# Neighbour sums by one-hot products: second pass in groups of four, its running counts on GpSimd, and keys read from PSUM

## The chip, the cores and the metric

One core of one Trainium2 chip. The metric is the device time of one execution in microseconds, the median over runs. Engines are called by the names of the profile: PE is TensorE's matmul side, PEld its weight loads, DVE VectorE, ACT ScalarE, POOL GpSimd, SP the engine that issues most DMAs.

## What is computed

A graph has 4096 nodes with 128 features each and 65536 edges. Each edge adds the features of its source node to the output row of its destination node:

```python
num_nodes, num_edges, dim = 4096, 65536, 128
output = np.zeros((num_nodes, dim), dtype=np.float32)
for i in range(len(edge_index_src)):
    output[edge_index_dst[i]] += node_features[edge_index_src[i]]
```

Source and destination indices are drawn at random. In and out are float32.

## The kernel before

The output is cut into 32 blocks of 128 destination nodes, the features into 32 blocks of 128 source nodes. The kernel sorts the edges by destination block and then by source block, so that each pair of blocks gets 128 edge places or a fixed part of them, and builds from the sorted edges a 128 x 128 matrix of counts for each pair. The output is then a sum of plain matrix products: counts times features. `_fast` (L79) holds all of it, in an order written out by hand; every engine runs its instructions in that order.

**Pass 1** (L312 to L492) sorts by destination block. The edges come as 24 chunks (NCH) by 22 (NJ), in six quarters q of four chunks. For a quarter, `oh1s` (L208) compares keys with a row of numbers and gives one-hots over 32 blocks; `counts` (L227) makes running counts with matmuls and ScalarE and gathers each edge's rank; `spread1` (L257) multiplies the one-hots by two payloads, the code of the edge (k = 0) and its source block (k = 1); `move1` (L275) builds a one-hot of the ranks on VectorE and multiplies it, on PE, with the spread payloads, so that each edge moves to its rank. The spread tile v1 has two buffers, used in turn by the quarters. `onehot` (L197) is the helper of all these comparisons, so they stand under L200 in the profile; its first operand (`piota`, `piotas`) lies in PSUM, in the tile `psi`. The first four destination blocks of the second pass are prepared beside the quarters (`beside`, L432). `x_part` (L182) splits the features in two parts that are multiplied separately: ScalarE rounds one, GpSimd subtracts for the other.

**Pass 2** (`pass2`, L506) sorts the edges of a group of destination blocks by source block. GROUPS gives the groups: 4, 4, 4, 4, 8 and 8 destination blocks. A group of four makes bucket one-hots (`buckets4`, one VectorE instruction), column sums, scans, and counts with 24 matmuls and six ScalarE passes (`counts_ranks`, L621). A group of eight makes them with 32 small VectorE instructions (`buckets`), sums on PE over all chunks before (`before_all`), 11 dependent VectorE additions (`running`, L553) and 12 GpSimd products (`masked`, L560). Both gather ranks with 32 matmuls (`ranks`), build permutations on VectorE (`permutations`) and apply them on PE to payloads that GpSimd multiplied (`payload`, `permuted`). ScalarE then takes the sorted keys out of PSUM (`take_pairs`, L408) to an SBUF tile `pa`, and VectorE extracts from it source and destination within the block (`put_keys`, L416, two instructions at L421). `little` hands out the GpSimd products, seven to a slot.

**The slots** (L720 to L746), one for each destination block, run beside that. In slot n VectorE makes the one-hots of slot n + 1 (`onehots`, L650: 2 x 4096 elements), PE multiplies this slot's one-hots to blocks of counts (`blocks`, L660: 8 of 4 matmuls each, in four PSUM buffers `psa`), ScalarE casts each to SBUF (L665), and PE multiplies the blocks of the slot before with the features (`product`, L667: 8 of 2 matmuls). After every fourth slot `evacuate` and `finish` (L295 to L310) copy the result out of PSUM, transpose it on PE and send it to HBM. STEPS says which steps of which group are taken in which slot; a step's first function runs after the one-hots, its second at the slot's end, its third two slots later.

```python
        for k0 in (0, 4):
            for k in range(k0, k0 + 4):
                blocks(k, cur, a)
            if k0 == 4:
                finish()
            if prev is not None:
                for k in range(k0, k0 + 4):
                    product(k, *prev)
```

Of the kernel before, what the change touches and what calls it, by code (L numbers as in the profile page):

```python
# [25 lines left out]
GROUPS = (4, 4, 4, 4, 8, 8)  # L26

STEPS = {0: (1, 2), 1: (1,), 2: (2,), 3: (3,), 4: (2,), 5: (3, 2), 6: (4,), 7: (4,), 8: (3,),
         9: (3,), 10: (4,), 12: (4,), 13: (4,), 14: (5,), 15: (5,), 16: (4,), 17: (4,), 18: (5,),
         20: (5,), 21: (5,), 24: (5,), 25: (5,)}  # L30
# [48 lines left out]
def _fast(ctx, tc, X, src32, dst32, out, ident, fmax, flag_i, T):  # L79
# [52 lines left out]
    psi = ps.tile([P, 4, P // 2], I32, name="psi", tag="psi", bufs=1)  # L132
# [124 lines left out]
    def spread1(q):  # L257
# [224 lines left out]
    for q in range(NQ):  # L482
# [15 lines left out]
    small = []  # L498

    def little(n=0, until=None):  # L500
        while small and (n > 0 or any(k == until for k, _ in small)):
            small.pop(0)[1]()
            n -= 1


    def pass2(g):  # L506


        d0, gd = first[g], GROUPS[g]
        kk = 4 if gd % 4 == 0 else 2  # L510
        gk = gd // kk
        shape = [P, NCH, gk, NB, kk]
        W = NB * gd
        T2 = {}

        def flat2(t):
            return t.rearrange("p c i s k -> p c (i s k)")

        def tiles():
            at = -(g - 1) % 3  # L520
            tags = ("c0", "o1", "o0")
            T2["o"] = sb1.tile(shape, BF16, name="oh2", tag=tags[at])[:]
            T2["c"] = sb1.tile(shape, BF16, name="cum2", tag=tags[(at + 1) % 3])[:]
            T2["v"] = sb1.tile(shape, BF16, name="v2", tag="F" if g % 2 == 0 else "c1")[:]

        def buckets():
            tiles()
            ds = slice(d0, d0 + gd)
            for s in range(NB):
                V.tensor_single_scalar(  # L530
                    out=T2["o"][:, :, :, s, :], scalar=float(s + 1), op=OP.is_equal,
                    in_=sbk[:, :, ds].rearrange("p c (i k) -> p c i k", k=kk))

        def before_all():
            psb = ps.tile([P, 512], F32, name="psb", tag="misc", bufs=1)
            for h in range(2):
                for c in range(NH):
                    PE.matmul(out=psb[:, h * W:(h + 1) * W], lhsT=before[:],
                              rhs=flat2(T2["o"])[:, h * NH + c], start=c == 0, stop=c == NH - 1)
            for h in range(2):  # L540
                S.copy(out=flat2(T2["c"])[:, h * NH], in_=psb[:, h * W:(h + 1) * W])  # L541

        def payload(i, cs):
            ds = slice(d0 + kk * i, d0 + kk * i + kk)
            G.tensor_tensor(out=T2["v"][:, cs, i], in0=T2["o"][:, cs, i], op=OP.mult,  # L545
                            in1=sa[:, cs, None, ds].to_broadcast([P, cs.stop - cs.start, NB, kk]))

        def payloads():
            for i in range(gk):
                for c in range(0, NCH, 4):  # L550
                    small.append(((g, 1), lambda i=i, c=c: payload(i, slice(c, c + 4))))

        def running():  # L553
            cums = flat2(T2["c"]).rearrange("p (h c) w -> p h c w", h=2)
            ohs2 = flat2(T2["o"]).rearrange("p (h c) w -> p h c w", h=2)
            for c in range(1, NH):
                V.tensor_tensor(out=cums[:, :, c], in0=cums[:, :, c - 1], in1=ohs2[:, :, c - 1],  # L557
                                op=OP.add)

        def masked():  # L560
            for c in range(0, NCH, 2):
                small.append(((g, 0), lambda c=c: G.tensor_tensor(  # L562
                    out=flat2(T2["c"])[:, c:c + 2], in0=flat2(T2["c"])[:, c:c + 2],
                    in1=flat2(T2["o"])[:, c:c + 2], op=OP.mult)))

        def ranks():
            little(until=(g, 0))
            psr = ps.tile([P, 512], F32, name="psr2", tag="misc", bufs=1)
            for s in range(NB):
                PE.matmul(out=psr[:, :NCH * gd], lhsT=identb[:],  # L570
                          rhs=T2["c"][:, :, :, s, :].rearrange("p c i k -> p (c i) k"),
                          start=s == 0, stop=s == NB - 1)
            T2["r"] = sb2.tile([P, gd // 2, NCH, 2, 2], BF16, name="rank2")
            for k in range(2):
                S.copy(out=T2["r"][:, :, :, :, k],
                       in_=psr[:, :NCH * gd].rearrange("p (c j u) -> p j c u", j=gd // 2, u=2))

        def permutations(i):
            pair_onehot(p2b[(d0 + i) // 2 % 4], T2["r"][:, i // 2], slice(0, NCH))

        def permuted(i):
            little(until=(g, 1))
            if i % 4 == 0:
                T2["ps2"] = ps.tile([P, 512], F32, name="ps2", tag="ps2", bufs=1)
            ps2 = T2["ps2"]
            for c in range(NCH):
                at = (c // NH * 2 + i % 4 // 2) * 64
                PE.matmul(out=ps2[:, at:at + 64], lhsT=p2b[(d0 + i) // 2 % 4][:, c, :],  # L588
                          rhs=T2["v"][:, c, i // kk, :, i % kk:i % kk + 2],
                          start=c % NH == 0, stop=c % NH == NH - 1)  # L590
            if i % 4 == 2:
# [250 lines left out]
```

## Time and profile before

| | us |
|---|---|
| median of 3 runs | 336.03 (334.42 to 336.85) |
| the profiled execution | 334.62 |
| its span, first to last instruction | 332.6 |
| PE busy | 280.8 (84%) |
| DVE busy | 283.4 (85%) |
| ACT busy | 199.8 (60%) |
| POOL busy | 94.7 (28%) |

The profile is of one execution. Busy time is the time in which an engine has an instruction at work; PE's ends are modelled, and POOL's are rough. Pass 1 goes to about 84 us of the span, the slots from about 90 to 327. DMA moves 5.76 MB and is busy almost only in the first 20 us. The mean granted clock of TensorE was 0.957 of 2.4 GHz.

### The profile page before, as it was taken

The page shows a single profiled execution, that of the slowest core. Times are in us where ns is not written, and L with a number is a line of the kernel's source. Part 1 is how long each engine was busy: PE and PEld are TensorE (multiplying, and loading weights), DVE is VectorE, ACT ScalarE, POOL GpSimd, SP SyncE. Part 2 cuts the span into 40 slices and gives each one's busy share as a digit, 9 for nine tenths or more (in the row PEclk, how much of TensorE's full clock was granted, in tenths as well). Part 3 has the DMA queues.
Part 4 walks back from the last instruction along what each step waited for, and adds up shares of the span by engine and source line. Part 5 has one row for each costly group of instructions (what it writes and reads, how often), then busy time and mean ns, then how long its engine had stood idle before and what let it go on. Part 6 is the DMA issues. An engine that isn't in the chain of part 4 may idle for free.

```text
span 332.6 us, 8069 instructions
## 1 busy us (share of the span) xinstructions
PE 280.8 (84%) x3488; PEld 235.0 (71%) x3496; DVE 283.4 (85%) x335; ACT 199.8 (60%) x411; POOL 94.7 (28%) x102
## 2 busy tenths in 40 slices
PE   0579868666739989899689999985999999999994
PEld 0468757656638778688478888864888888888882
DVE  4999999977899839958999899999989969968800
ACT  2776545311735867865547578562657787787761
POOL 6634021110606070003999000189920000000000
PEclk9999999969878999999979999995999999999999
DMA  8500000000000000100001001000100100100101
GB/s 240 138 2 5 2 3 2 2 2 2 2 3 0 2 3 0 34 3 0 2 0 34 2 0 34 0 2 1 34 2 0 34 2 0 34 0 3 34 1 32
DMA packets 8708, 5.76 MB, mean 17 GB/s; under 512 B 224, under 2 KB 8416, under 8 KB 8672
## 3 DMA queue, kind: packets, MB, share of 16 engines
q1 hardware_dynamic: 8528, 4.72, 5.0%
q8 instruction: 27, 0.44, 0.6%
q10 hardware_dynamic: 144, 0.52, 0.5%
q14 instruction: 9, 0.07, 0.1%
HBM read 3.15 MB, written 2.10 MB: 16 GB/s over the span
## 4 chain that ended last, share of the span: by engine, by line
PE 51%; DVE 36%; issue 6%; ACT 4%; DMA 1%; DVEq 0%; ACTq 0%
PE pso L670 27%; PE psa L663 14%; DVE oh L200 12%; DVE p L200 6%; DVE v L261 5%; DVE cum L557 5%; PE ps L588 3%; PE psr L570 3%; ACT cum L631 2%; DMA raw<-in_edge_index_dst_dram 1%; DVE p2a L200 1%; DVE oh L530 1%; PE psm L285 1%; DVE oh L602 1%; DVE p2c L200 1%
## 5 line engine op out<-in xcount | busy, mean ns | idle before, releaser
L665 ACT CAST a<-psa 128x512 fp32r<-128x512 f32 x256 | 131.6, 605 | 48.9 <-PE psa L663 48.3
L670 PE MATMUL pso<-a,xr 128*128 128x512 f32 x512 | 135.0, 406 | 0.0
L670 PEld LDWEIGHTS pso<-a,xr 128*128 128x128 f32 x512 | 93.0, 191 | 17.2
L200 DVE TENSOR_TENSOR oh<-psi,slo 128x4096 bf16<-128x4096 uint16 (+1 forms) x33 | 73.3, 2221 | 20.2 <-PE psa L663 20.1
L200 DVE TENSOR_TENSOR oh<-psi,dlo 128x4096 bf16<-128x4096 uint16 (+1 forms) x33 | 73.1, 2216 | 0.0
L663 PE MATMUL psa<-oh 128*128 128x128 bf16 x1024 | 70.8, 224 | 0.5 <-DVE oh L200 0.3
L663 PEld LDWEIGHTS <-oh 128*128 128x128 bf16 x1024 | 60.2, 100 | 12.0 <-issue 10.9
L545 POOL TENSOR_TENSOR v<-oh,sa 128x512 bf16<-128x512 bf16 x42 | 42.6, 1054 | 35.2 <-DVE oh L602 35.2
L562 POOL TENSOR_TENSOR cum<-cum,oh 128x512 bf16<-128x512 bf16 x24 | 29.5, 1252 | 65.8 <-DVE cum L557 65.8
L200 DVE TENSOR_TENSOR p<-psi,rank 128x448 bf16<-128x448 uint16 (+3 forms) x72 | 29.7, 474 | 0.0
L240 ACT ACTIVATE cum<-psc,minus 128x512 bf16<-128x512 f32 (+1 forms) x36 | 21.4, 653 | 11.8 <-PE psc L237 11.7
L285 PE MATMUL psm<-v,p 128*128 128x64 bf16 x512 | 20.8, 197 | 2.1 <-DVE p L200 1.8
L588 PE MATMUL ps<-v,p2c 128*128 128x64 bf16 x192 | 8.7, 209 | 14.1 <-DVE p2c L200 14.1
L285 PEld LDWEIGHTS <-p 128*128 128x128 bf16 x512 | 18.4, 101 | 2.8 <-DVE p L200 2.6
L588 PEld LDWEIGHTS <-p2c 128*128 128x128 bf16 x192 | 7.6, 107 | 16.5 <-DVE p2c L200 15.2
L557 DVE TENSOR_TENSOR cum<-cum,oh 128x512 bf16<-128x512 bf16 x22 | 16.1, 732 | 1.5 <-ACT cum L541 0.8
L189 POOL TENSOR_TENSOR xr<-xf,xr 128x512 fp32r<-128x512 f32 x8 | 11.9, 1519 | 12.9 <-ACT xr L185 12.9
L358 POOL TENSOR_TENSOR vc<-oh,sa 128x512 bf16<-128x512 bf16 x5 | 5.2, 1048 | 33.9 <-DVE oh L353 33.9
L200 DVE TENSOR_TENSOR p2a<-psi,rank 128x3072 bf16<-128x3072 uint16 (+2 forms) x14 | 14.5, 1062 | 0.2 <-ACT rank L390 0.2
L215 PE MATMUL pst<-ones,oh 128*128 128x1 bf16 x132 | 4.3, 164 | 12.0 <-DVE oh L200 12.0
L237 PE MATMUL psc<-identb,sums 128*128 128x128 bf16 x126 | 13.9, 234 | 0.4 <-issue 0.2
L237 PEld LDWEIGHTS <-sums 128*128 128x128 bf16 x126 | 11.1, 106 | 4.5 <-issue 1.4
(94 smaller groups left out, 278.1 us busy)
## 6 DMA issues: line engine op xcount, KB each, us to landing
xf<-in_node_features_dram SPq DMA_DIRECT2D x4, 512.0 KB, 7.4
out_dram<-rows SPq DMA_DIRECT2D x8, 256.0 KB, 2.3
raw<-in_edge_index_src_dram ACTq DMA_DIRECT2D x1, 512.0 KB, 4.7
raw<-in_edge_index_dst_dram SPq DMA_DIRECT2D x1, 512.0 KB, 5.0
```

The costliest lines, as they stand in the source:

```text
L200: V.tensor_tensor(out=dst.rearrange("p i (m k) -> p i m k", k=2), in0=io.rearrange("p i (m k) -> p i m k", k=2), in1=keys2[:, :, None, :]. ...
L237: PE.matmul(out=psc[:, (j - j0) * P:(j - j0 + 1) * P], lhsT=sums[q][:, j - 1:j].to_broadcast([P, P]), rhs=identb[:], start=False, stop=j = ...
L240: S.activation(out=cum[:, :, 4 * j0:4 * (j0 + n)], func=RELU, bias=minus[:], in_=psc[:, :n * P].rearrange("p (t b) -> p b t", b=NB))
L261: V.tensor_tensor(out=v1[q][:, :, k, :].rearrange("p t (b k) -> p t b k", k=2), in0=oh1q(q).rearrange("p t (b k) -> p t b k", k=2), in1=ke ...
L285: PE.matmul(out=psm[:, l * 64:(l + 1) * 64], lhsT=t[:, l % 2, j, :], rhs=v1[q][:, 4 * j + l].rearrange("p k b -> p (k b)"), start=j == 0, ...
L545: G.tensor_tensor(out=T2["v"][:, cs, i], in0=T2["o"][:, cs, i], op=OP.mult, in1=sa[:, cs, None, ds].to_broadcast([P, cs.stop - cs.start, N ...
L557: V.tensor_tensor(out=cums[:, :, c], in0=cums[:, :, c - 1], in1=ohs2[:, :, c - 1], op=OP.add)
L562: small.append(((g, 0), lambda c=c: G.tensor_tensor(out=flat2(T2["c"])[:, c:c + 2], in0=flat2(T2["c"])[:, c:c + 2], in1=flat2(T2["o"])[:, ...
L588: PE.matmul(out=ps2[:, at:at + 64], lhsT=p2b[(d0 + i) // 2 % 4][:, c, :], rhs=T2["v"][:, c, i // kk, :, i % kk:i % kk + 2], start=c % NH = ...
L663: PE.matmul(out=psa[:, i * P:(i + 1) * P], lhsT=oh[:, 0, 4 * k + i, :], rhs=oh[:, 1, 4 * k + i, :], start=True, stop=True)
L665: S.copy(out=a[:, k, :], in_=psa[:])
L670: PE.matmul(out=pso[:], lhsT=xr[s // 16][:, s % 16, v, :], rhs=a[:, k, :], start=s == 0 and v == 0, stop=s == NB - 1 and v == 1)
```

## The change

- Pass 1: `spread1` is split. `spread_blocks` multiplies the source blocks (k = 1) on GpSimd, four instructions of 22 x 32 elements a quarter. `spread_codes` keeps the codes (k = 0) on VectorE; it first copies the quarter's keys, as 88 fp32 words, to PSUM (`pkey`) and reads them from there. The subtraction of the third part of the features moves behind the first two `spread_blocks` in GpSimd's order.
- The PSUM tile of `psi` becomes a full bank. Behind the numbers for the comparisons lie `pkey` and two buffers `pa`.
- `take_pairs` writes the sorted keys as fp32 to `pa` in PSUM, and `put_keys` reads the upper 16 bits of each word there.
- Pass 2: eight groups of four. Group 0 is made in pass 1 as before, group 1 with column sums and counts as before, groups 2 to 7 with one bucket instruction, `before_all`, 11 additions of 2 x 128 elements (`running`, now on GpSimd), six masks of 512 and six payloads of 512, all on GpSimd and given out at once. `little` goes.
- STEPS: group g from 3 on takes its steps in slots 4g - 9 (buckets, sums), 4g - 8 (running, masked, payloads), 4g - 6 (ranks), 4g - 4 and 4g - 3 (permutations); its keys are extracted in slot 4g - 1, where the one-hots of slot 4g are made.
- The slots: the products of a slot's first four groups of blocks follow its last four blocks, and those of its last four follow the next slot's first four blocks.

```diff
-GROUPS = (4, 4, 4, 4, 8, 8)
+GROUPS = (4,) * 8
+
+STEPS = {0: (2,), 1: (1, 1, 2), 3: (2,), 4: (2,), 5: (2,)}
+for _g in range(3, 8):
+    for _s in (4 * _g - 9, 4 * _g - 8, 4 * _g - 6, 4 * _g - 4, 4 * _g - 3):
+        STEPS[_s] = STEPS.get(_s, ()) + (_g,)
...
+    psib = ps.tile([P, 512], I32, name="psi", tag="psi", bufs=1)
+    psi = psib[:, :4 * P // 2].rearrange("p (n w) -> p n w", w=P // 2)
+    pkey = psib[:, 512 - 3 * 4 * NJ:].rearrange("p (n w) -> p n w", w=4 * NJ)
...
-        for k, key in ((0, kab), (1, kb[:])):
-            V.tensor_tensor(
-                out=v1[q][:, :, k, :].rearrange("p t (b k) -> p t b k", k=2),
-                in0=oh1q(q).rearrange("p t (b k) -> p t b k", k=2),
-                in1=key[:, q, :, None, :].to_broadcast([P, NL, NB // 2, 2]), op=OP.mult)
+        for l in range(4):
+            G.tensor_tensor(out=v1[q][:, l::4, 1, :], in0=oh1q(q)[:, l::4], op=OP.mult,
+                            in1=kb[:, q, l::4, :1].to_broadcast([P, NJ, NB]))
+
+    def spread_codes(q):
+
+        V.tensor_copy(out=pkey[:, q % 3].bitcast(F32),
+                      in_=ka[:, q].rearrange("p t k -> p (t k)").bitcast(F32))
+        V.tensor_tensor(
+            out=v1[q][:, :, 0, :].rearrange("p t (b k) -> p t b k", k=2),
+            in0=oh1q(q).rearrange("p t (b k) -> p t b k", k=2), op=OP.mult,
+            in1=pkey[:, q % 3].bitcast(BF16).rearrange("p (t k) -> p t k", k=2)[:, :, None, :]
+            .to_broadcast([P, NL, NB // 2, 2]))
...
     oh1s(2)
+    spread_blocks(0)
     x_part(2, 0)
-    x_part(2, 1)
     count(0)
-    spread1(0)
+    spread_codes(0)
...
     count(1)
+    spread_blocks(1)
     x_part(3, 0)
+    x_part(2, 1)
     x_part(3, 1)
...
+    pa = [psib[:, 256 + i * P:256 + (i + 1) * P].bitcast(F32) for i in range(2)]
...
-        pau = pa[:].bitcast(U16).rearrange("p s d -> p (s d)")[
-            :, :, None].to_broadcast([P, 4 * NB, 2])
+        pau = pa.bitcast(U16).rearrange("p (n w) -> p n w", w=2)[:, :, 1:].to_broadcast([P, 4 * NB, 2])
...
+        if q + 2 < NQ:
+            spread_blocks(q + 2)
         if q + 1 < NQ:
-            spread1(q + 1)
+            spread_codes(q + 1)
...
+            T2["o"] = sb1.tile([P, NCH, NB, 4], BF16, name="oh2", tag=("o1", "c0")[g % 2])
+            T2["c"] = sb1.tile([P, NCH, NB, 4], BF16, name="cum2", tag="o0")
+            T2["v"] = sb1.tile([P, NCH, NB, 4], BF16, name="v2", tag=("F", "c1")[g % 2])
...
             for c in range(1, NH):
-                V.tensor_tensor(out=cums[:, :, c], in0=cums[:, :, c - 1], in1=ohs2[:, :, c - 1],
-                                op=OP.add)
+                G.tensor_tensor(out=cum[:, :, c], in0=cum[:, :, c - 1], in1=oh[:, :, c - 1], op=OP.add)
...
         def masked():
-            for c in range(0, NCH, 2):
-                small.append(((g, 0), lambda c=c: G.tensor_tensor(
-                    out=flat2(T2["c"])[:, c:c + 2], in0=flat2(T2["c"])[:, c:c + 2],
-                    in1=flat2(T2["o"])[:, c:c + 2], op=OP.mult)))
+            for c in range(0, NCH, 4):
+                G.tensor_tensor(out=flat("c")[:, c:c + 4], in0=flat("c")[:, c:c + 4],
+                                in1=flat("o")[:, c:c + 4], op=OP.mult)
...
-        if gd == 4:
-            return [(both(buckets4, payloads), column_sums), (sums_to_each, counts_ranks)] + pairs
-        return [(buckets, before_all), (both(running, masked, payloads),),
+        if g == 1:
+            return [(each(buckets, payloads), column_sums), (sums_to_each, counts_ranks)] + pairs
+        return [(buckets, before_all), (each(running, masked, payloads),),
                 (lambda: None, ranks)] + pairs
...
-        for k0 in (0, 4):
-            for k in range(k0, k0 + 4):
-                blocks(k, cur, a)
-            if k0 == 4:
-                finish()
-            if prev is not None:
-                for k in range(k0, k0 + 4):
-                    product(k, *prev)
-        if prev is not None and prev[0] % 4 == 3:
-            evacuate(prev[0] // 4, prev[2])
+        for k in range(4):
+            blocks(k, cur, a)
+        if prev is not None:
+            for k in range(4, 8):
+                product(k, *prev)
+            if prev[0] % 4 == 3:
+                evacuate(prev[0] // 4, prev[2])
+        for k in range(4, 8):
+            blocks(k, cur, a)
+        for k in range(4):
+            product(k, slot, a, pso)
+        finish()
...
-    for k in range(8):
+    for k in range(4, 8):
         product(k, *prev)
```

## Rows read from the trace of the kernel before

**Rows 1.** Busy by stage: stretch, length, then PE, PEld, DVE, ACT, POOL; clock.
```profile
51.30:59.50 8.20, 6.49 (x130) 5.28 (x129) 8.20 (x18) 5.89 (x13) 1.05 (x1) 1.00 0.01 2
...
149.00:168.70 19.70, 15.58 (x149) 12.77 (x148) 18.52 (x17) 9.36 (x19) 13.28 (x11) 0.98 0.00 1
...
188.70:230.00 41.30, 35.89 (x350) 29.62 (x350) 40.96 (x60) 24.99 (x51) 13.49 (x11) 0.95 0.03 8
...
257.50:327.30 69.80, 69.74 (x655) 57.18 (x652) 50.86 (x33) 50.13 (x101) 0.00 (x0) 1.00 0.04 13
```

**Rows 2.** The chain of waits in order of time: start us, us, what.
```profile
84.47 1.09 DVE slo L421
...
86.61 3.90 DVE oh L200 x4
91.22 4.47 DVE oh L200 x2
...
97.28 1.75 DVE oh L602
...
99.88 1.73 PE psa L663 x16
...
106.97 0.73 PE ps L588 x24
...
117.42 1.53 PE psr L570 x32
...
300.54 0.91 PE psa L663 x16
...
306.16 0.91 PE psa L663 x16
...
309.89 0.44 PE psx L304 x4
...
327.28 0.59 ACT res L297
```

**Rows 3.** Groups by line on DVE: busy us, mean ns, idle before.
```profile
L557 DVE TENSOR_TENSOR cum<-cum,oh 128x512 bf16<-128x512 bf16 x22 | 16.1, 732 | 1.5 <-ACT cum L541 0.8
L261 DVE TENSOR_TENSOR v<-oh,ka 128x2816 bf16<-128x2816 bf16 x6 | 11.1, 1856 | 0.0
L421 DVE TENSOR_SCALAR slo<-pa 128x256 uint16<-128x256 uint16 x8 | 10.9, 1362 | 2.4 <-ACT pa L414 2.4
L261 DVE TENSOR_TENSOR v<-oh,kb 128x2816 bf16<-128x2816 bf16 x6 | 10.7, 1791 | 0.0
...
L200 DVE TENSOR_TENSOR oh<-psi,kd 128x2816 bf16<-128x2816 uint16 x6 | 9.6, 1603 | 0.0
```

**Rows 4.** Timeline of DVE: start us, us, instruction, idle before and its releaser.
```profile
27.43 2.65 DVE L261 TENSOR_TENSOR v<-oh,ka 128x2816 bf16<-128x2816 bf16 x1
...
72.14 0.18 DVE L367 TENSOR_TENSOR_SCAN sums<-ones,pst 128x12 bf16<-128x12 bf16 x1 [1.77 <-ACT rank L390]
...
109.67 0.28 DVE L421 TENSOR_SCALAR slo<-pa 128x256 uint16<-128x256 uint16 x1
...
161.26 2.28 DVE L200 TENSOR_TENSOR oh<-psi,slo 128x4096 bf16<-128x4096 uint16 x1
...
178.07 4.33 DVE L421 TENSOR_SCALAR slo<-pa 128x256 uint16<-128x256 uint16 x1
```

**Rows 5.** Timeline of POOL.
```profile
27.33 3.88 POOL L189 TENSOR_TENSOR xr<-xf,xr 128x512 fp32r<-128x512 f32 x2 [5.42 <-ACT xr L185]
...
160.97 9.20 POOL L562 TENSOR_TENSOR cum<-cum,oh 128x512 bf16<-128x512 bf16 x8 [0.36 <-DVE cum L557]
170.13 12.12 POOL L545 TENSOR_TENSOR v<-oh,sa 128x512 bf16<-128x512 bf16 x12
```

**Rows 6.** Timeline of PE, the sums of the first group of eight.
```profile
149.32 2.79 PE L538 MATMUL psb<-oh,before 128*128 128x256 bf16 x24
```

**Rows 7.** Timeline of ACT, the first of three copies of sorted keys.
```profile
107.74 0.44 ACT L412 CAST pa<-ps 64x128 bf16<-64x128 f32 x1 [1.25 <-PE ps L588]
```

More of the change, by code (lines that the diff above doesn't have):

```diff
@@ L490, in _fast @@
             oh1s(q + 4)
+        if q + 2 < NQ:
+            spread_blocks(q + 2)
         if q + 1 < NQ:
-            spread1(q + 1)
+            spread_codes(q + 1)
     first = [sum(GROUPS[:g]) for g in range(len(GROUPS))]
[L498 to L503, printed above, removed]
-    def pass2(g):
[L509 to L513, printed above, removed]
+    def pass2(g):
+        d0 = first[g]
@@ L526, in buckets, with flat @@
+            T2["c"] = sb1.tile([P, NCH, NB, 4], BF16, name="cum2", tag="o0")
+            T2["v"] = sb1.tile([P, NCH, NB, 4], BF16, name="v2", tag=("F", "c1")[g % 2])
+        def flat(k, h=None):
+            t = T2[k][:].rearrange("p c s k -> p c (s k)")
+            return t if h is None else t.rearrange("p (h c) w -> p h c w", h=2)
         def buckets():
             tiles()
[L528 to L532, printed above, removed]
+            V.tensor_tensor(
+                out=T2["o"][:], op=OP.is_equal,
+                in0=psi[:, 2].bitcast(U16).rearrange("p (s k) -> p s k", k=4)[
+                    :, None].to_broadcast([P, NCH, NB, 4]),
+                in1=sbk[:, :, None, d0:d0 + 4].to_broadcast([P, NCH, NB, 4]))
@@ L534, in before_all, with payloads @@
+        def payloads():
+            for c in range(0, NCH, 4):
+                G.tensor_tensor(out=T2["v"][:, c:c + 4], in0=T2["o"][:, c:c + 4], op=OP.mult,
+                                in1=sa[:, c:c + 4, None, d0:d0 + 4].to_broadcast([P, 4, NB, 4]))
         def before_all():
             psb = ps.tile([P, 512], F32, name="psb", tag="misc", bufs=1)
[L536 to L551, printed above, removed]
+            for c in range(NCH):
+                h = c // NH
+                PE.matmul(out=psb[:, h * P:(h + 1) * P], lhsT=before[:], rhs=flat("o")[:, c],
+                          start=c % NH == 0, stop=c % NH == NH - 1)
@@ L560, in masked @@
         def masked():
[L561 to L564 removed]
+            for c in range(0, NCH, 4):
+                G.tensor_tensor(out=flat("c")[:, c:c + 4], in0=flat("c")[:, c:c + 4],
+                                in1=flat("o")[:, c:c + 4], op=OP.mult)
         def ranks():
[L567 removed]
@@ L568, in ranks @@
             psr = ps.tile([P, 512], F32, name="psr2", tag="misc", bufs=1)
[L569 to L573, printed above, removed]
+            for b in range(NB):
+                PE.matmul(out=psr[:, :4 * NCH], lhsT=identb[:], rhs=T2["c"][:, :, b, :],
+                          start=b == 0, stop=b == NB - 1)
@@ L574, in ranks @@
+            T2["r"] = sb2.tile([P, 2, NCH, 2, 2], BF16, name="rank2")
             for k in range(2):
                 S.copy(out=T2["r"][:, :, :, :, k],
[L576 to L583, printed above, removed]
+                       in_=psr[:, :4 * NCH].rearrange("p (c j u) -> p j c u", j=2, u=2))
@@ L584, in permuted, with permutations @@
+        def permutations(j):
+            pair_onehot(p2b[d0 // 2 % 4 + j], T2["r"][:, j], slice(0, NCH))
+        def permuted(j):
+            if j == 0:
                 T2["ps2"] = ps.tile([P, 512], F32, name="ps2", tag="ps2", bufs=1)
@@ L630, in counts_ranks, with each @@
                               start=False, stop=c == cs[-1])
[L631 removed]
+                S.activation(out=flat("c")[:, c0:c0 + 4].rearrange("p c w -> p (c w)"),
                              in_=psc[:], func=RELU, bias=minus[:])
             ranks()
[L635 to L646 removed]
+        def each(*fs):
+            return lambda: [f() for f in fs]
+        pairs = [(lambda: permutations(0), lambda: permuted(0)),
+                 (lambda: permutations(1), lambda: permuted(1), quad_keys)]
+        if g == 1:
+            return [(each(buckets, payloads), column_sums), (sums_to_each, counts_ranks)] + pairs
+        return [(buckets, before_all), (each(running, masked, payloads),),
                 (lambda: None, ranks)] + pairs
```

62 lines of the change are left out of this document (16 added, 46 removed).

## The prediction, from the trace of the kernel before

> **What bounds the kernel now.** I read the busy times by stage first. In pass 1 VectorE is the full engine: from 51.3 to 59.5 us it is busy 8.20 of 8.20 us, TensorE 6.49 [rows 1]. In pass 2 two kinds of stage stand beside each other. From 257.5 to the end TensorE is busy 69.74 of 69.80 us. From 149.0 to 168.7 and from 188.7 to 230.0 VectorE is the full one (18.52 of 19.70, 40.96 of 41.30) and TensorE stands idle for 4.1 and 5.4 us [rows 1].
>
> The chain of waits, in order of time, gives the floor of pass 2. In the undisturbed end one slot (8 groups of blocks, 16 products) goes from 300.54 to 306.16: 5.62 us, all TensorE [rows 2]. Slot 1 starts at 99.88 and the last product ends at 327.28, so 227.4 us go to 31 slots that at 5.62 would take 174.2, with one slot's products (3.8) behind them. The 49 us left are permutations, ranks, counts, and stalls. The groups by line name the stalls' makers: 22 running-count adds on VectorE (16.1 us) and the key extractions, which take 0.28 when nothing is in their way and average 1.36 [rows 3, 4].
>
> Why they are slow is in the timelines. VectorE's spread, with two inputs in SBUF, takes 2.65 at 27.43, beside GpSimd's subtractions, where the six of a kind average 1.86 with this one in them; two subtractions take 3.88 there. A key extraction that starts at 178.07 lasts 4.33, until the GpSimd burst of 170.13 has ended at 182.25, against 0.28 with GpSimd idle [rows 3 to 5]. The one-hot at 161.26, with one input in PSUM, takes its usual 2.2 to 2.3 beside a burst [rows 2, 4, 5].
>
> **Pass 1.** Removed from VectorE: one of two spreads in each of six quarters. The pairs cost 11.1 + 10.7 = 21.8 us [rows 3]. Left are six spreads with the key in PSUM and six copies of 88 words into PSUM. A copy is about an extraction of 256 elements, 0.28 [rows 4]; I take 0.3. The spread with its key as second operand in PSUM is not in the trace. Without the pair at 27.43 one takes (21.8 - 2 x 2.65) / 10 = 1.65. Bounds for the new one: 1.6 as now, or half the rate, 3.2. The one-hot of the same 2816 elements with its first operand in PSUM averages 1.60 (9.6 us for six), the same as both in SBUF [rows 3], so I take 1.6. VectorE: 21.8 - 6 x 1.9 = 10.4 us less.
>
> The Trainium skill speaks against this: VectorE: DVE Perf Modes, section "The perf-mode tier table", lists tensor_tensor at 1x for any operand in PSUM. By that the six spreads would be twice as long and the sum 312; the one-hot row disagrees for the first operand, and no run here shows the second.
>
> Not all of it reaches the end. The stage of 8.2 shrinks by 1.3 (1.6 less 0.3) to 6.9, while TensorE's 6.49 [rows 1] stay, in order, with ScalarE's ranks between them, so TensorE begins to be waited for. From nothing to all of it could go; I choose 0.4 for each of six quarters, 2.4. Pass 1 gives 8 us.
>
> GpSimd takes 24 products of 704 elements. By its payload row (12.12 for 12 of 512, so 1.01) one is 1.39; by its mask row (9.20 for 8, 1.15) 1.58; by the subtraction next to a two-input VectorE op (1.94) 2.67 [rows 5]. No such op runs beside it any more, so I take 1.5, 6.0 a quarter. A quarter's products start when its buffer's earlier matmuls end and are wanted when the next quarter is through, some 9 us later (6.9, the spread and the first one-hots); with one payload of 1.0 queued ahead that is 7.0. They fit, by 2 us. The subtractions of blocks 2 and 3 now queue behind two such quarters; their result is first used in slot 2, some 60 us later: no cost. At 2.67 they would not fit.
>
> **From pass 1 to slot 1.** The extractions of slot 0's keys take 84.47 to 86.61, beside GpSimd; from PSUM 0.55. Then 4.6 for slot 0's one-hots, 4.47 for slot 1's, 1.7 for the next four's bucket one-hots (1.75 now) [rows 2]; the permutation that stood before these, up to 97.28, moves to slot 1. Then 24 sums of 128 columns, half of the 2.79 that 24 of 256 took [rows 6]: 1.4. Slot 1 at 84.47 + 0.55 + 4.6 + 4.47 + 1.7 + 1.4 = 97.2 instead of 99.88: 2.7 less. Half of slot 0's products lie in TensorE's wait there.
>
> **Slots 1 to 31.** TensorE: 31 x 5.62 = 174.2; four last products less than now, so 1.9 behind it; 14 permutations at 0.73 = 10.2; 6 ranks at 1.53 = 9.2; 5 more sums at 1.4 = 7.0; 7 transposes at 0.44 = 3.1 [rows 2, 6]. That is 205.6. In slot 3 ranks and sums stand next to each other in one PSUM buffer, and the sums wait for ScalarE's two copies: 0.9. Sum 206.5, if nobody else is later.
>
> VectorE per four slots: 8 one-hots of 2.2 = 17.6, buckets 1.7, two permutations 3.4, keys and maximum 0.8: 23.5, against TensorE's 4 x 5.62 + 0.44 + 1.46 + 1.53 + 1.4 = 27.3. The running counts go from VectorE altogether. The cover is not free, though. The new place of the keys is in the PSUM bank that every one-hot reads, and ScalarE writes it. The trace shows what sharing a bank does: a scan waited 1.77 us for ScalarE's copy of other columns of its bank [rows 4]. So the one-hots two slots ahead, which could start during the slot, wait until the permutation's matmuls and ScalarE's three copies (the first takes 0.44 [rows 7], I take 1.2 for all) are done, 1.4 into the next slot; then 4.4 for one-hots, ready at 5.8. They are wanted at 5.62 + 1.53 = 7.15, since that slot ends with ranks. Hidden with 1.3 to spare; the buckets after them come at 12.5 and are wanted at 12.8. I add 0.3 for each of six groups. Slots: 208.3 instead of 227.4, 19.1 less.
>
> The Trainium skill, PSUM - Partial Sum Buffer, section "PSUM bank collisions raise a hardware error", wants any two engines kept apart on one bank and quadrant, whatever the columns; the scan row agrees.
>
> GpSimd per four: 11 dependent adds of 256 elements, 6 masks at 1.15, 6 payloads at 1.01 [rows 5]. No row has 256: from 0.51 (half a payload) to 1.15 (no cheaper than a mask). I take 0.7, with the wait on the one before. 7.7 + 6.9 + 6.1 = 20.7 of 27.3. Adds and masks (14.6) have from a slot's start to the end of the third slot, 18.8 (three slots, two permutations, the transposes), less under 1 for the copy they start from, an estimate from the 0.44 of a like one.
>
> Products half a slot later than their blocks add no wait: blocks 4 to 7 already need the buffers that casts 0 to 3 free.
>
> **Sum.** The profiled execution took 334.62 us, span 332.6. 334.62 - 8 - 2.7 - 19.1 = 304.8; behind the last product nothing changes. The median shown, 336.03, is 1.4 above this execution. I predict 305.
>
> **Rivals.**
> - The spread with a PSUM key runs at half rate: 6 x 1.6 = 9.6 of the 10.4 go back, 7.2 of the 8 at the end: 312. For it: no row of the form; against: the one-hot at full rate.
> - GpSimd bounds pass 1: at over 2 us a product the quarters wait for it, 5 to 8 us in all: 310 to 313. For it: the subtractions at 1.94; against: the bursts at 1.0 to 1.15.
> - GpSimd bounds pass 2: at 1.15 an add, plus 0.25 for each wait, 15.4 + 6.9 + 6.1 = 28.4 a group, beyond 27.3, and ranks late by up to 5 in the first and 1 to 2 in later groups: 309 to 320. Against: large ops on GpSimd grow about with size.
> - The shared bank costs more: each of six sets of copies 2 to 3 us later than I have it, behind casts on ScalarE, puts 1 to 2 us into the path: 311 to 317.
> - Slower than before: the copy of keys into PSUM is held off by GpSimd as the extraction at 178.07 was. Its source is in SBUF, and a GpSimd burst of four products is always about when it comes. Six copies, each a burst of 6 us: 305 + 36 = 341. It decides from 5.2 us each. Against: an extraction has both ends in SBUF, this copy only one, as the one-hots, which were never held.
> - The gain of pass 2 is not there because TensorE is full anyway: it would then be pass 1's 8 + 2.7, about 324. Against: the idle 4.1 and 5.4 us, and the counts on TensorE that go.
>
> **How the numbers follow.** Forecast 0.60 (299 to 311), the PSUM key 0.06, GpSimd in pass 1 0.07, GpSimd in pass 2 0.13, the bank 0.06, no gain in pass 2 0.02, slower 0.04, quicker still (pass 1 gives all 10.4) 0.02. The range 298 to 320 takes the first five (0.92) and leaves out less than 2 in 10, with room for prices that no row bounds. A measurement of this kernel tells about 1% from no change; all but two cases are faster by more: faster 0.93, same 0.02, slower 0.05.
>
> **What would show it.** Right: spreads at 1.6 with the key in PSUM; extractions at 0.3; TensorE busy nearly throughout from slot 4, four slots in 27 to 28 us; the idle before one-hots named after ScalarE's key copies without a later wait of TensorE for one-hots. Wrong: TensorE's ranks waiting for GpSimd masks; its quarter matmuls waiting for GpSimd spreads; key copies over 1 us. The prediction falls if adds on GpSimd take over 1.1, or if the order of pass 1 leaves TensorE behind VectorE by more than 2 us a quarter.

## Result: 302.8 us

The changed kernel takes 302.81 us (median of 4; 301.93 to 303.05), the kernel before 335.49 (334.42 to 336.85) beside it on the same chip. The ratio is 0.9019 with a 95% interval of 0.8979 to 0.906. Forecast were 305 us and 298 to 320.

The page of the kernel after: its span and the busy times of the engines, then the chain that ended last, by engine.

```profile
span 301.3 us, 8172 instructions
...
PE 272.4 (90%) x3552; PEld 229.5 (76%) x3552; DVE 249.6 (83%) x251; ACT 191.5 (64%) x405; POOL 180.8 (60%) x204
...
PE 74%; DVE 19%; ACT 3%; DMA 2%; issue 1%; DVEq 0%
```

TensorE is now busy 90% of the span, and three quarters of the chain lie on it. By stage, with the columns of [rows 1]: a quarter of pass 1, four slots of pass 2, and the end.

```profile
46.83:53.93 7.10, 6.79 (x141) 5.78 (x139) 6.96 (x18) 5.26 (x12) 6.49 (x5) 1.00 0.01 3
166.40:193.44 27.04, 27.04 (x304) 22.96 (x301) 23.52 (x15) 18.69 (x40) 20.18 (x23) 1.00 0.04 12
226.10:295.90 69.80, 69.31 (x678) 57.34 (x676) 51.27 (x34) 49.81 (x102) 15.54 (x17) 1.00 0.04 13
```

In pass 1 VectorE still is the full engine (6.96 of 7.10), with TensorE close behind it (6.79). In pass 2 TensorE no longer stands idle: 27.04 of 27.04, where the middle of the kernel before had VectorE full and TensorE idle for 4 to 5 us of a stretch. GpSimd, nearly unused in pass 1 before, works 6.5 of 7.1 us and 20.2 of 27.0.

The chain of waits, where it answers to [rows 2]: slot 0's key extraction and one-hots, slot 1's one-hots, its sums and its first blocks; the double permutation; then ranks and sums of a later period, and the end.

```profile
77.54 0.42 DVE slo L434
...
78.30 4.53 DVE oh L203 x4
82.90 4.00 DVE oh L203 x2
87.29 1.76 DVE oh L530
89.10 1.50 PE psb L545 x24
90.60 0.89 PE psa L639 x16
...
96.20 1.52 PE ps L578 x48
...
158.06 1.39 PE psr L562 x32
...
165.05 1.36 PE psb L545 x24
166.40 0.89 PE psa L639 x16
...
291.70 3.73 PE pso L646 x16
```

Three differences of time between the two profiled executions hold the whole gain. Slot 0's key extraction starts at 77.54 instead of 84.47: 6.9 us from pass 1. From there to slot 1 it takes 13.06 instead of 15.41: 2.35. From slot 1 to the end of the last product it takes 204.8 (90.60 to 295.43) instead of 227.4: 22.6. Together that is 31.9; the tail behind the last product is 5.9 instead of 5.3, which leaves the 31.3 between the two spans.

What the moved and the new operations cost, by line and form (busy us, mean ns of one, idle before), answering to [rows 3]:

```profile
L271 DVE TENSOR_TENSOR v<-oh,psi 128x2816 bf16<-128x2816 bf16 x6 | 9.7, 1621 | 0.4
L269 DVE COPY psi<-ka 128x88 f32<-128x88 f32 x6 | 1.5, 251 | 0.2
L434 DVE TENSOR_SCALAR slo<-psi 128x256 uint16<-128x256 uint16 x8 | 3.3, 417 | 0.9 <-ACT psi L428 0.9
L264 POOL TENSOR_TENSOR v<-oh,kb 128x704 bf16<-128x704 bf16 x24 | 32.9, 1401 | 5.2 <-issue 2.7
L552 POOL TENSOR_TENSOR cum<-cum,oh 128x256 bf16<-128x256 bf16 x66 | 44.4, 672 | 39.3 <-ACT cum L547 34.6
```

The spread with its key in PSUM takes 1.62, the copy that feeds it 0.25. The extraction averages 0.42, where it averaged 1.36. GpSimd's work for one group of four, from its timeline (the columns of [rows 4]):

```profile
193.98 8.18 POOL L552 TENSOR_TENSOR cum<-cum,oh 128x256 bf16<-128x256 bf16 x11 [6.07 <-ACT cum L547]
202.12 6.76 POOL L556 TENSOR_TENSOR cum<-cum,oh 128x512 bf16<-128x512 bf16 x6
208.84 6.08 POOL L538 TENSOR_TENSOR v<-oh,sa 128x512 bf16<-128x512 bf16 x6
```

An add takes 0.74 with the wait for the one before it. The three pieces make 21.0 us of a period of 27.0, and GpSimd is idle for 6.07 before the next.

### The profile page after: what moved, and what is told of

Same layout as the page of the kernel before. It is cut to its first block, busy times and chain, and to the rows that moved or that the text cites. A ratio compares the mean times of both kernels' runs of the same rounds, so it can differ in the third digit from the quotient of the medians.

```text
span 301.3 us, 8172 instructions
## 1 busy us (share of the span) xinstructions
PE 272.4 (90%) x3552; PEld 229.5 (76%) x3552; DVE 249.6 (83%) x251; ACT 191.5 (64%) x405; POOL 180.8 (60%) x204
## 4 chain that ended last, share of the span: by engine, by line
PE 74%; DVE 19%; ACT 3%; DMA 2%; issue 1%; DVEq 0%
PE pso L646 40%; PE psa L639 19%; DVE p L203 6%; DVE oh L203 5%; PE ps L578 3%; PE psb L545 3%; PE psr L562 3%; DVE v L271 2%; ACT cum L243 2%; DMA raw<-in_edge_index_dst_dram 2%; PE psm L296 2%; DVE kd L166 1%; PE psx L315 1%; DVE oh L530 1%; PE psr L248 1%
## 5 line engine op out<-in xcount | busy, mean ns | idle before, releaser
L646 PE MATMUL pso<-a,xr 128*128 128x512 f32 x512 | 133.6, 403 | 0.0
L646 PEld LDWEIGHTS pso<-a,xr 128*128 128x128 f32 x512 | 91.6, 189 | 16.6
L203 DVE TENSOR_TENSOR oh<-psi,slo 128x4096 bf16<-128x4096 uint16 (+1 forms) x33 | 73.3, 2222 | 25.4 <-ACT psi L428 23.2
L639 PE MATMUL psa<-oh 128*128 128x128 bf16 x1024 | 68.5, 220 | 0.4
L552 POOL TENSOR_TENSOR cum<-cum,oh 128x256 bf16<-128x256 bf16 x66 | 44.4, 672 | 39.3 <-ACT cum L547 34.6
L639 PEld LDWEIGHTS <-oh 128*128 128x128 bf16 x1024 | 58.1, 98 | 10.4 <-issue 9.9
L556 POOL TENSOR_TENSOR cum<-cum,oh 128x512 bf16<-128x512 bf16 x36 | 40.6, 1166 | 0.0
L264 POOL TENSOR_TENSOR v<-oh,kb 128x704 bf16<-128x704 bf16 x24 | 32.9, 1401 | 5.2 <-issue 2.7
L296 PE MATMUL psm<-v,p 128*128 128x64 bf16 x512 | 19.7, 197 | 0.0
L236 PE MATMUL psc<-oh,early 128*128 128x512 bf16 (+1 forms) x36 | 14.3, 396 | 0.0
L203 DVE TENSOR_TENSOR p2c<-psi,rank 128x3072 bf16<-128x3072 uint16 x8 | 13.9, 1751 | 0.0
L218 PEld LDWEIGHTS <-oh 128*128 128x128 bf16 x132 | 3.8, 99 | 12.7 <-DVE oh L203 12.7
```

The costliest lines, as they stand in the source:

```text
L203: V.tensor_tensor(out=dst.rearrange("p i (m k) -> p i m k", k=2), in0=io.rearrange("p i (m k) -> p i m k", k=2), in1=keys2[:, :, None, :]. ...
L236: PE.matmul(out=psc[:, :n * P], lhsT=early[:], rhs=oh1q(q)[:, 4 * j0:4 * (j0 + n), :].rearrange("p t b -> p (t b)"), start=True, stop=j0 + ...
L264: G.tensor_tensor(out=v1[q][:, l::4, 1, :], in0=oh1q(q)[:, l::4], op=OP.mult, in1=kb[:, q, l::4, :1].to_broadcast([P, NJ, NB]))
L296: PE.matmul(out=psm[:, l * 64:(l + 1) * 64], lhsT=t[:, l % 2, j, :], rhs=v1[q][:, 4 * j + l].rearrange("p k b -> p (k b)"), start=j == 0, ...
L552: G.tensor_tensor(out=cum[:, :, c], in0=cum[:, :, c - 1], in1=oh[:, :, c - 1], op=OP.add)
L556: G.tensor_tensor(out=flat("c")[:, c:c + 4], in0=flat("c")[:, c:c + 4], in1=flat("o")[:, c:c + 4], op=OP.mult)
```

## Experiments

Each edit is made to the changed kernel, except in the last but one, and each ratio is against the kernel before. Undoing a part tells what it is worth there: the numbers don't add up to the total, since parts lean on each other.

### Both spreads back on VectorE, keys in SBUF

```diff
-        for l in range(4):
-            G.tensor_tensor(out=v1[q][:, l::4, 1, :], in0=oh1q(q)[:, l::4], op=OP.mult, ...)
...
+        for k, key in ((0, kab), (1, kb[:])):
+            V.tensor_tensor(out=v1[q][:, :, k, :]..., in0=oh1q(q)...,
+                in1=key[:, q, :, None, :].to_broadcast([P, NL, NB // 2, 2]), op=OP.mult)
```

> The changed kernel with the spreads of pass 1 back on VectorE, both with keys in SBUF; GpSimd does none. Theory (the split shortened pass 1): VectorE gets 10 us back in pass 1, the collision of the last three key shifts with GpSimd (3.52 us in the changed kernel, 2.31 before) eases by 1.2, and the changed kernel's key extraction at 77.54 comes some 7 us later: 308 to 311 us. Rival (TensorE's order set pass 1, and its shortening comes from elsewhere): 302 to 305 us.

Measured: 309.07 us, 0.9232 (0.9206 to 0.9257), so 6.3 us of the gain hang on this part. The extraction starts at 84.06, 6.5 later. The first spread in this kernel meets GpSimd's subtractions again, as in [rows 4]:

```profile
27.45 2.65 DVE L268 TENSOR_TENSOR v<-oh,ka 128x2816 bf16<-128x2816 bf16 x1
```

### The code spread's key read from SBUF

```diff
-        V.tensor_copy(out=pkey[:, q % 3].bitcast(F32), in_=ka[:, q]...)
...
-            in1=pkey[:, q % 3].bitcast(BF16)...
+            in1=kab[:, q, :, None, :].to_broadcast([P, NL, NB // 2, 2]))
```

> The changed kernel with the code spread on VectorE reading its key from SBUF, without the copy to PSUM; the GpSimd spreads stay. Theory (two SBUF inputs on VectorE and a GpSimd instruction hold each other up): VectorE saves six copies of 0.28 and loses about 1 us in each spread that meets a GpSimd burst, five of six: 304 to 307 us; if a spread waits until a whole burst of four or eight has ended, the first alone loses 12 us: 312 us and more. Rival (the place of the key does not matter): 301 to 302.5 us.

Measured: 305.40 us, 0.9126 (0.9098 to 0.9154), 2.6 more than the changed kernel. Its spreads by line (least, middle and longest ns, where they lie, form), then GpSimd's first two bursts in its timeline:

```profile
L269 DVE TENSOR_TENSOR v<-oh,ka x6: 2342/2568/2827, 17.4 to 61.1; 128x2816 bf16<-128x2816 bf16 x6
```

```profile
14.38 12.32 POOL L264 TENSOR_TENSOR v<-oh,kb 128x704 bf16<-128x704 bf16 x8
```

A spread takes 2.57 instead of 1.62, and GpSimd's eight products, beside one of them, 12.32 where the changed kernel has 10.94. So with both inputs in SBUF both engines lose where they meet, VectorE 0.95 us and GpSimd 1.4: VectorE is held for less than one GpSimd product (1.4), not for a burst of 5.5. The Trainium skill says (SBUF - State Buffer, section "Who interferes with whom") that a VectorE instruction with two SBUF inputs contends with a GpSimd instruction that reads SBUF. The trace agrees: 2.57 us against 1.62.

### Running counts back on VectorE, groups of four

```diff
-                G.tensor_tensor(out=cum[:, :, c], in0=cum[:, :, c - 1], in1=oh[:, :, c - 1], op=OP.add)
+                V.tensor_tensor(out=cum[:, :, c], in0=cum[:, :, c - 1], in1=oh[:, :, c - 1], op=OP.add)
```

> The changed kernel with the 11 additions of running counts of groups 2 to 7 on VectorE. They take some 3 us a group there. Theory (VectorE has no room in pass 2 although it shows 3.5 us of idle time a group, since that idle time is a wait for ScalarE's key copies which in turn wait for VectorE's permutations): the loop of VectorE's 26.8 us, the permutation's matmuls 0.73 and the copies with their waits 1.4 is 28.9 a group instead of 27.0, so about 2 us a group more: 311 to 316 us. Rival (the regrouping in fours did it, the engine does not matter, the idle time takes the additions in): 302 to 304 us.

Measured: 323.98 us, 0.9683 (0.9649 to 0.9716): 21.2 us of the 32.7 are lost. The direction was expected, the size was not (311 to 316). VectorE's timeline shows the adds of one group, and the same one-hot of two periods:

```profile
149.47 5.23 DVE L552 TENSOR_TENSOR cum<-cum,oh 128x256 bf16<-128x256 bf16 x11
...
162.45 2.29 DVE L203 TENSOR_TENSOR oh<-psi,slo 128x4096 bf16<-128x4096 uint16 x1 [1.69 <-ACT psi L428]
...
192.78 2.29 DVE L203 TENSOR_TENSOR oh<-psi,slo 128x4096 bf16<-128x4096 uint16 x1 [1.69 <-ACT psi L428]
```

The eleven adds take 5.23, not the 3 that I had put down. The reason is in their single times: here are all 66 (least, middle and longest ns, where they lie, form), then GpSimd's first masks beside the eleven above, in its timeline.

```profile
L552 DVE TENSOR_TENSOR cum<-cum,oh x66: 276/293/1143, 96.4 to 246.7; 128x256 bf16<-128x256 bf16 x66
```

```profile
150.87 1.20 POOL L556 TENSOR_TENSOR cum<-cum,oh 128x512 bf16<-128x512 bf16 x1 [16.12 <-DVE cum L552]
152.96 1.26 POOL L556 TENSOR_TENSOR cum<-cum,oh 128x512 bf16<-128x512 bf16 x1 [0.89 <-DVE cum L552]
```

Nine adds of a group take 0.3 each, about what I had put down. The two others take 1.14, and each runs beside a GpSimd mask: in this group they start at 151.09 and 153.24, while the two masks shown are running. So of the 5.23 some 3.5 are the adds and their waits for each other, and 1.7 is the meeting with the masks. The kernel before has the same, with four of the eleven adds of each group of eight:

```profile
L557 DVE TENSOR_TENSOR cum<-cum,oh x22: 418/426/1280, 152.9 to 222.0; 128x512 bf16<-128x512 bf16 x22
```

VectorE's 23.5 us a period become 28.7, past TensorE's 27.0, and the period is 30.3. Without the meeting they would be 27.0 (an estimate, 28.7 less 1.7). The 1.6 left over is the wait of 1.69 for ScalarE's key copies, whose cause a later run takes up.

### Sorted keys in SBUF in pass 2

```diff
-    pa = [psib[:, 256 + i * P:256 + (i + 1) * P].bitcast(F32) for i in range(2)]
+    pas = [sb1.tile([P, 4 * NB], BF16, name=f"pa{i}") for i in range(2)]
+    pa = [t[:] for t in pas]
```

> The changed kernel with the sorted keys in an SBUF tile of bf16, as before the change. VectorE then doesn't wait for ScalarE (23.2 us over seven groups in the changed kernel), and the key extraction reads SBUF. Theory (the extraction is held until the GpSimd burst that runs beside it has ended): it waits some 6 us a group, of which about 3.5 is what VectorE no longer waits for ScalarE; the one-hots come about 3 us later than in the changed kernel and TensorE waits for them by 2 us a group, with 1.5 more at slot 0: 309 to 318 us. Rival (the shared bank is the dearer of the two): 299 to 302 us.

Measured: 305.36 us, 0.9119 (0.9081 to 0.9157), between the theory and its rival. Extractions in VectorE's timeline, the first slot's pair and one of pass 2:

```profile
77.90 1.10 DVE L435 TENSOR_SCALAR slo<-pa 128x256 uint16<-128x256 uint16 x1 [1.12 <-ACT pa L429]
...
183.03 0.75 DVE L435 TENSOR_SCALAR slo<-pa 128x256 uint16<-128x256 uint16 x1
183.70 1.14 DVE L435 TENSOR_SCALAR dlo<-pa 128x256 uint16<-128x256 uint16 x1
```

GpSimd holds these extractions for about one instruction, not for 4.33 as in [rows 4]: of all sixteen, the fourteen beside its work take 0.69 to 1.25, the last two, with GpSimd idle, 0.28. In the loop VectorE has 3.5 us a period to spare, and that hides it; in slot 0 nothing does, and slot 1 starts at 92.35 instead of 90.60. That is 1.75 of the 2.5 us lost; the rest I have not followed. So the keys in PSUM are worth little here, and the theory that pass 2 needs them falls. In the kernel before, too, the pair at 84.47 beside a burst takes 1.09 and 1.14; why two others (4.33 and 4.05 us) lasted to the end of a burst, four GpSimd instructions later, is open.

### Sorted keys in another PSUM bank

```diff
-                take_pairs(pa[g % 2], ps2[:, :8 * NB])
+                T2["pa"] = ps2[:, 256:384]
+                take_pairs(T2["pa"], ps2[:, :8 * NB])
```

> The changed kernel with the sorted keys of groups 1 to 7 in the free half of the PSUM tile that the permutations' matmuls write, so that ScalarE's copies no longer share a bank with the one-hots' first operand. Theory (the waits on the shared bank are hidden): VectorE's 23.2 us of waiting for ScalarE's key copies go, TensorE's path stays, 302 to 303.5 us. Rival (the bank delays one-hots that TensorE needs): 298 to 301.5 us.

Measured: 302.89 us, 0.9036 (0.9014 to 0.9059), 0.1 from the changed kernel. The waits of VectorE's one-hots (us in all, times, longest) in the changed kernel, then in this one:

```profile
DVE oh L203 <- ACT psi L428: 23.2, 7, 3.9
```

```profile
DVE oh L203 <- PE psa L640: 24.1, 25, 2.5
```

23.2 us of waiting for ScalarE's copies are gone, and 24.1 us of waiting for the blocks that free a one-hot's buffer have come for them. VectorE's idle time belongs to the period, whatever it is put down to: sharing the bank costs nothing that can be measured here. In all these runs the keys that share a bank with the one-hots' operand also share a tile with it, so the runs do not tell which of the two the waits follow.

### Products in the order of before

```diff
-        for k in range(4):
-            blocks(k, cur, a)
...
+        for k0 in (0, 4):
+            for k in range(k0, k0 + 4):
+                blocks(k, cur, a)
+            if k0 == 4:
+                finish()
+            if prev is not None:
+                for k in range(k0, k0 + 4):
+                    product(k, *prev)
...
-    for k in range(4, 8):
+    finish()
+    for k in range(8):
```

> The changed kernel with the products a whole slot behind their blocks, as before the change. Theory (the order only moves four products of 1.9 us from TensorE's wait in slot 0 to the end): 304 to 305.5 us. Rival (the half slot frees casts and buffers and takes stalls out of every slot): above 307 us. Rival (no effect): 302 to 303.5 us.

Measured: 306.34 us, 0.9122 (0.909 to 0.9154), 3.5 more, between the theory and the larger rival. The products at the end take 5.54 instead of 3.73, which is the 1.8 that was expected. The rest was not: the busy times around slot 0's end (columns as above), in the changed kernel and in this one.

```profile
87.00:89.00 2.00, 1.71 (x8) 1.18 (x7) 2.00 (x3) 1.35 (x3) 0.00 (x0) 1.00 0.00 0
89.00:92.00 3.00, 2.90 (x43) 2.82 (x43) 3.00 (x3) 1.31 (x4) 0.73 (x2) 1.00 0.03 5
```

```profile
87.00:89.00 2.00, 0.00 (x0) 0.00 (x0) 2.00 (x2) 1.48 (x4) 0.00 (x0) 1.00 0.00 0
89.00:92.00 3.00, 2.78 (x27) 2.78 (x27) 3.00 (x3) 0.00 (x0) 0.00 (x0) 0.52 0.02 5
```

Half of slot 0's products fill TensorE's wait in the changed kernel. Without them it is idle from 87 to 89, and the granted clock of the next 3 us is 0.52, near the lower of its two levels (1.2 of 2.4 GHz), instead of 1.00. The 24 sums take 2.72 there instead of 1.50, and slot 1 starts at 91.94 instead of 90.60. So of 3.5 us the order itself is 1.8, the slower stretch 1.3; the last 0.4 lies behind the last product (6.27 us to the end of the span against 5.87) and is open. The mean granted clock of the six runs goes with their time: 0.982 in two of 304.4 us, 0.967 to 0.974 in four of 306.2 to 306.9. The trace is of one of the four.

### All key shifts first

```diff
-    for q in range(3):
+    for q in range(NQ):
...
-    for q in range(3, NQ):
-        dst_keys(q)
```

> The changed kernel with all six quarters' key shifts ahead of the first one-hots, before GpSimd's first subtraction, so that the last three (3.52 us in the changed kernel) no longer meet GpSimd. Theory (this collision is the 1.2 us by which pass 1 fell short, and VectorE is the path there): VectorE 2 to 3 us earlier at its third one-hot, of which the wait for ranks lets through about 1: 301 to 302.3 us. Rival (TensorE and ScalarE set the time there): 302.5 to 303.5 us.

The question was where the first quarter's gain went: its one-hots start at 21.04, no earlier than the 20.90 of before, though one spread is gone ahead of them. Three key shifts take 3.52 in the changed kernel, beside GpSimd's first products. Measured: 303.74 us, 0.9064 (0.9041 to 0.9088), no better, and above what theory and rival had. The six shifts take 1.26 here, but in VectorE's timeline two others lose it:

```profile
9.14 1.66 DVE L174 SCALAR_TENSOR_TENSOR raw<-raw 128x528 uint16<-128x528 uint16 x1
...
19.77 0.20 DVE L227 TENSOR_TENSOR_SCAN sums<-ones,pst 128x22 bf16<-128x22 bf16 x1 [1.45 <-PE pst L218]
```

The code operation takes 1.66 instead of 0.71, and the scan waits 1.45 for TensorE's column sums. The first one-hots start at 21.76. The shifts were the place where the loss showed, not its cause.

### Scans of quarters 3 and 4 later

In the changed kernel the scan of quarter 3 waits for TensorE, in VectorE's timeline:

```profile
33.33 0.20 DVE L227 TENSOR_TENSOR_SCAN sums<-ones,pst 128x22 bf16<-128x22 bf16 x1 [1.28 <-PE pst L218]
```

```diff
-            if l == 1:
-                if q + 3 < NQ:
-                    scan(q + 3)
...
+            if l == (3 if q < 2 else 1) and q + 3 < NQ:
+                scan(q + 3)
```

> The changed kernel with the scans of quarters 3 and 4 at the end of a quarter's four one-hots instead of behind the second, so that VectorE does not wait there for TensorE's column sums (1.28 us at 33.33 in the changed kernel). Theory (VectorE is the path through that quarter): 301.0 to 302.2 us. Rival (TensorE and ScalarE are the path there, and pass 1 fell short of its 10 us by their order): 302.4 to 303.6 us.

Measured: 302.16 us (median of 6), 0.9004 (0.8977 to 0.903).

```profile
34.43 0.18 DVE L227 TENSOR_TENSOR_SCAN sums<-ones,pst 128x22 bf16<-128x22 bf16 x1
...
76.17 0.42 DVE L434 TENSOR_SCALAR slo<-psi 128x256 uint16<-128x256 uint16 x1 [0.90 <-ACT psi L428]
```

The wait is gone, the extraction starts 1.37 earlier, and slot 1 at 89.22 instead of 90.60. So this wait took 1.3 us of pass 1's gain, as the trace shows it. In time this version can't be told from the changed kernel: the two intervals overlap, so theory and rival stay undecided by the time alone.

### The kernel before, its running counts on GpSimd in groups of eight

This edit is made to the kernel before: GpSimd instead of VectorE for the adds of L557, nothing else.

```diff
-                V.tensor_tensor(out=cums[:, :, c], in0=cums[:, :, c - 1], in1=ohs2[:, :, c - 1],
+                G.tensor_tensor(out=cums[:, :, c], in0=cums[:, :, c - 1], in1=ohs2[:, :, c - 1],
```

> The kernel before with one edit: the 11 additions of running counts of the two groups of eight on GpSimd. Nothing is regrouped. Theory (the adds' place on VectorE makes the two stalls of pass 2): VectorE gets 16.8 us back, TensorE's two idle stretches go, GpSimd's chain of 11 adds of 1.25 and 12 masks of 1.15 is late for the ranks by up to 3 us in each group: 318 to 326 us. Rival (groups of eight are too coarse for GpSimd, and only the regrouping lets the adds move): 329 to 337 us.

Measured: 331.28 us, 0.9892 (0.9855 to 0.9929), in the rival's range. GpSimd's timeline, then the chain:

```profile
153.99 13.57 POOL L557 TENSOR_TENSOR cum<-cum,oh 128x512 bf16<-128x512 bf16 x11 [29.11 <-ACT cum L541]
167.51 13.55 POOL L562 TENSOR_TENSOR cum<-cum,oh 128x512 bf16<-128x512 bf16 x12
```

```profile
181.11 4.07 PE psr L570 x32
...
226.61 13.53 POOL cum L562 x12
240.18 2.81 PE psr L570 x32
```

For a group of eight the adds and the masks are one piece of 27.1 us, and TensorE's ranks wait for its end, 3.7 us in each of the two groups. The move to GpSimd alone brings about 4 us; all the rest of the change without the move brings about 11 (to 324.0, third experiment); both together 32.7. Neither stands for the gain by itself: the fours cut GpSimd's piece to 14.9 (8.18 + 6.76), which three slots cover: in the changed kernel the masks of the group shown above end at 208.84, and TensorE's ranks start at 212.12. The two moves are not of one size, though: the kernel before has 22 adds on VectorE (16.1 us), the fours put 66 there (31.4).

### Running counts on VectorE, keys in another bank

The edits of the third and the fifth experiment together:

```diff
-                G.tensor_tensor(out=cum[:, :, c], ...
+                V.tensor_tensor(out=cum[:, :, c], ...
...
+                T2["pa"] = ps2[:, 256:384]
```

> The changed kernel with the running counts on VectorE (as in the run that took 323.98) and with the sorted keys of groups 1 to 7 in the bank of the permutations' matmuls, so that VectorE does not wait for ScalarE's copies. Theory (VectorE, TensorE's permutation and ScalarE's copies form a loop of 30.3 us a group because of the shared bank): the loop opens by the 1.7 us that VectorE waits for ScalarE in each group, VectorE's own 28.6 to 28.9 a group is left: 312 to 317 us. Rival (VectorE's work alone sets the 30.3): 322 to 325 us.

Measured: 317.59 us, 0.9455 (0.9422 to 0.9488), 6.4 less than with the shared bank, just above the theory's 317 and well below the rival's 322. The same extraction of two periods, in VectorE's timeline:

```profile
165.13 0.41 DVE L434 TENSOR_SCALAR slo<-ps 128x256 uint16<-128x256 uint16 x1
...
194.15 0.41 DVE L434 TENSOR_SCALAR slo<-ps 128x256 uint16<-128x256 uint16 x1
```

The period is 29.0 instead of 30.3, close to VectorE's 28.7. The same sharing that costs nothing that can be measured when VectorE has 3.5 us a period to spare costs 6.4 over the kernel when it has none.

## Why the prediction was right, step by step

The mechanism held at each of its three places, and the sum (304.8) came out 2 us above the median measured. None of the signs that would have shown it wrong is there: TensorE's ranks wait for no mask, a spread on GpSimd takes 1.40 busy and 1.37 in a burst, a key copy takes 0.25. The sum is closer than its terms, and that is luck in part: pass 1, the way to slot 1 and the tail came 2.0 us short together (1.1, 0.35 and 0.55), the slots 3.5 better than forecast.

- **Pass 1: 8 forecast, 6.9 measured.** The spread with a PSUM key was put at 1.6 and took 1.62. VectorE's spreads cost 10.6 us less (21.8 - 9.7 - 1.5, forecast 10.4), but 3.7 of them were given back, not 2.4. Up to the first rank one-hots the gain is -0.1 us, then from quarter to quarter 3.2, -0.3, 1.7, 1.1 and 1.1, and 0.3 from there to the extraction. A steady quarter takes 7.1 (forecast 6.9). What the sum lacked is at the front: 1.3 us in which the scan waits for TensorE (gone in the trace of the run with later scans) and the first quarter's lost spread. The latter meets GpSimd and TensorE in turn, and the try to free it only moved the wait; what would free it stays open.
- **From pass 1 to slot 1: 2.7 forecast, 2.35 measured.** The extractions were put at 0.55 for two. From PSUM one takes 0.42, more than the 0.28 from SBUF that I scaled from; the 24 sums took 1.50 instead of 1.4.
- **Slots 1 to 31: 208.3 forecast, 204.8 measured**, the largest miss. Four slots take 27.03, not 27.3: ranks 1.39 instead of 1.53, sums 1.36 instead of 1.4. In slot 3 the wait between ranks and sums, in the chain, is 0.48 (from 110.36 to 110.84), not 0.9. The 0.3 a group for the shared bank is nothing that can be measured, as the fifth experiment shows.
- **GpSimd in pass 2.** An add was put at 0.7 and took 0.74, the group at 20.7 and took 21.0.
- **The makers of the stalls.** The prediction named two on VectorE, the adds and the key extractions. The adds are borne out by the third experiment, but not all of their 16.1 us was work: eight of the 22 were at 1.28 instead of 0.43 beside GpSimd's masks, 6.8 us in all. The extractions are not borne out for the changed kernel: with the keys back in SBUF they are held again, and four slots still take 27.0.

The bank wait came as forecast: the one-hots two slots ahead start when ScalarE's third key copy is done, and the wait is hidden. Here is one, with the copies that it waits for, in the timelines of VectorE and, below it, of ScalarE:

```profile
180.23 2.29 DVE L203 TENSOR_TENSOR oh<-psi,slo 128x4096 bf16<-128x4096 uint16 x1 [3.52 <-ACT psi L428]
```

```profile
179.52 0.23 ACT L426 COPY psi<-ps 64x128 f32<-64x128 f32 x1 [1.25 <-PE ps L578]
179.78 0.41 ACT L428 COPY psi<-ps 64x64 f32<-64x64 f32 x2
```

The three copies take 0.67, where I had 1.2. The one-hots end at 184.63, 1.9 before TensorE has done with the ranks (at 186.48) and wants them; forecast was 1.3. The rule on banks that I had cited from the Trainium skill (PSUM - Partial Sum Buffer, section "PSUM bank collisions raise a hardware error") agrees with the waits, as far as bank and tile go together here, and the fifth and the last experiment put what it costs at nothing that can be measured or at 6.4 us, by what hides it.

Of the rivals, the half-rate spread is excluded by its 1.62: by the Trainium skill (VectorE: DVE Perf Modes, section "The perf-mode tier table") it would have taken twice as long, and the trace disagrees for the second operand as it did for the first. GpSimd as the bound in either pass is excluded by its idle time, and "no gain in pass 2" by the 22.6 us. The key copy into PSUM held off by GpSimd, the rival of the other sign, is excluded by the copy's 0.25; and its price took a burst of 6 us as the unit of the hold, where the second and the fourth experiment show at most about one GpSimd instruction. Six of these, an estimate from the 1.4 of a product, are 8 us, which would not have turned the sign.

What the parts are worth, each undone alone: running counts on GpSimd 21.2 us, one spread on GpSimd and the other's key in PSUM 6.3 (the PSUM key alone 2.6), the order of products 3.5, sorted keys in PSUM 2.5.

## What to carry to other kernels

Before an engine's work is moved, compare the period of each engine after the move: here 5.2 us of adds on VectorE were the difference between 23.5 and 28.7 us beside a TensorE period of 27.0, and slower adds on GpSimd (0.74 against 0.3) were free. Count in what the two engines do to each other where they meet: 1.7 of the 5.2 us were that. Look at the longest unbroken piece that the move makes on the new engine and at what waits for its end: the move with pieces of 27 us brought 4 us, the larger move with pieces of 15 made no wait for a mask and is worth 21.2. A wait named in the profile is worth removing only if the waiting engine is short of time: 23.2 us of waits were removed and the time stayed as it was.

## What the runs showed that was not expected

- A dependent add of 256 elements takes 0.3 us on VectorE when nothing holds it and 0.74 on GpSimd, but in each group two of VectorE's eleven took 1.14 beside a GpSimd mask, so that eleven took 5.23 there and 8.18 on GpSimd, only 1.6 times as long.
- VectorE held by GpSimd, with all operands in SBUF, loses at most about one GpSimd instruction: 0.95 us for a spread, 0.4 to 1.0 for an extraction, 0.85 for an add. In two places of the kernel before it lost four instructions; why is open.
- 2 us without a matmul were followed by a granted clock of 0.52 for the next 3 us and by sums of 2.72 instead of 1.50 us. Not every pause is: in the run on the kernel before, TensorE paused 3.7 us ahead of each group of eight's ranks, and the granted clock was 0.54 in the next 3 us the first time (ranks 4.07) and 1.00 the second time (2.81).
- ScalarE's copies of keys from PSUM to PSUM take 0.19 to 0.24 us each, where the copy to SBUF of [rows 7] took 0.44; ScalarE's share of the bank wait was half of what I took.
